# A two-layer trunk on one core: residual by token, MLPs with stationary activations, the up projection as Strassen's 2x2 product run in turns with the down projection

## The chip, the core and the metric

The kernel runs on one core of a Trainium2 chip. The core has a matrix engine (TensorE, PE in the profile, its weight loads PEld), VectorE (DVE), ScalarE (ACT), GpSimd (POOL) and SyncE (SP), and 16 DMA engines behind queues that SP and POOL write to. The metric is device time in microseconds (us) of one execution; lower is better.

## The reference, cut to what matters

256 tokens, 2048 channels, 8192 MLP channels, all float32. Layer 0 mixes by pooling, layer 1 by stick-breaking attention with 16 heads of 128; both end in a squared-ReLU MLP.

```
def squared_relu_mlp(x, w_up, w_down):
    h = jax.nn.relu(jnp.einsum('bsd,df->bsf', x, w_up))
    return jnp.einsum('bsf,fd->bsd', h * h, w_down)

x = x + multiscale_pool_mixer(rms_norm(x, pool_norm[0]), pool_w[0], pool_scale[0])
x = x + squared_relu_mlp(rms_norm(x, mlp_norm[0]), w_up[0], w_down[0])
kv = rms_norm(x, kv_norm) @ w_kv                  # [256, 4096]
q = rms_norm(x, attn_norm[0]) @ w_q
x = x + stick_breaking_attention(q, k, v) @ w_o[0]
x = x + squared_relu_mlp(rms_norm(x, mlp_norm[1]), w_up[1], w_down[1])
return rms_norm(x, final_norm)
```

## The kernel before

All weights come as blocks of 1 MB: 512 input channels by 512 output channels, on chip `[128, 4, 512]`. There are 324: 4 for pooling, 64 up and 64 down for each layer, 48 for K, Q and V, 16 for the attention's output projection (o_w). The list `order` fixes their sequence, and `emit_block` takes them from it, three ahead of the one in use (`AHEAD`): a DMA on SP's queue into `raw` (four buffers), then ACT copies it rounded into `hi` (L117) and DVE writes the rest, `raw - hi`, into `lo` (L118), in halves of 1024 columns. Activations too are split in two, side by side in one tile (`xt`, `ht`, `oT`: 256 columns of the high part, 256 of the low). A product is the sum of three: high by high, high by low, low by high.

The residual stream `xs[n]` lies transposed: channels on the partitions, 256 tokens in the columns. Two functions multiply:

- `product_w`, for up, down, K, Q and o_w: pieces of the weights are stationary (loaded into PE) and the activations stream. Each of 16 pieces of a block takes a matmul of 512 columns with `hi` (L158) and one of 256 with `lo` (L163).
- `product_a`, for the pooling map and V: pieces of the activations are stationary and 512 weight columns stream, 24 matmuls for a block (L196 to L198).

An MLP goes in groups of `GF` = 2048 hidden channels (`NG` = 4): four column tiles of up, of four blocks each, then four of down. The evacuation of an up tile adds the halves, applies the token scale and ReLU, squares and splits (`squared_relu`). The evacuation of a down or o_w tile adds to `xs` (`add_to_stream`, L289 and L290); in the last group it also makes the next product's activations, pair by pair (`Norm.take`). The norm's factor, 1 / rms, is put on behind the product.

Matmul order on PE, the order on each queue and the buffers are as the code is written, apart from what stands in `high_priority`. The line numbers are those of the profile.

Of the kernel before, what the change touches and what calls it, by code (L numbers as in the profile page):

```python
# [2 lines left out]

# [20 lines left out]
GF = 2048  # L24
# [6 lines left out]
AHEAD = 3  # L31
WARM = 12
COLS = ("pool", "mlp0", "mlp1", "kv", "attn", "pool_scale", "final")


@with_exitstack
def trunk_kernel(ctx: ExitStack, tc: tile.TileContext, xt_in, band, cols, pool_w, up_w, down_w,
                 k_w, q_w, v_w, o_w, out):
    """The residual stream lies transposed on chip: xs[n] is [channel, channel tile, token]."""
    nc = tc.nc  # L40

    const = ctx.enter_context(tc.tile_pool(name="const", bufs=1))
    wraw = ctx.enter_context(tc.tile_pool(name="wraw", bufs=4))
# [35 lines left out]
    order = []  # L79
    for g in range(NCH):  # L80
        order.append((pool_w[g], None))

    def mlp_blocks(layer):
        for g in range(NG):
            for n in range(NCH):
                for kg in range(NCH):
                    order.append((up_w[layer, g * NCH + n, kg], None))
            for n in range(NCH):
                for kg in range(NCH):
                    order.append((down_w[layer, g, n, kg], None))  # L90
# [12 lines left out]
    state = {"emitted": 0, "used": 0}

    def emit_block():
        i = state["emitted"]
        src, gain = order[i]
        raw = wraw.tile([P, KT, NB], F32, name="raw")
        step = KT // 2 if i < NCH else KT
        for k in range(0, KT, step):  # L110
            nc.sync.dma_start(raw[:, k:k + step, :], src[:, k:k + step, :])
        hi = whi.tile([P, KT, NB], F32R, name="hi")
        lo = wlo.tile([P, KT, NB], F32R, name="lo")
        if gain is None:
            step = KT // 2
# [29 lines left out]
    def product_w(acts, evacuate, groups=NCH):  # L145
        """bank[j] = rows of output tile j of (W.T @ x_hi + W_lo.T @ x_hi | W_hi.T @ x_lo)"""
# [24 lines left out]
    def summed(new_pair, then):  # L171
        """Evacuation that hands on the sums of two tiles' halves."""
# [11 lines left out]

    def product_a(acts, evacuate, groups=NCH):
        """bank[t] = tokens t's rows of acts.T @ W"""
        banks = [ps_w.tile([P, NB], F32, name="bank") for _ in range(NT)]
        for kg in range(groups):
            hi, lo = next_block()
            for t in range(NT):  # L190
                for k in range(KT):
                    a_hi = acts[kg][:, k, t * P:(t + 1) * P]
                    a_lo = acts[kg][:, k, S + t * P:S + (t + 1) * P]
                    first = kg == 0 and k == 0
                    last = kg == groups - 1 and k == KT - 1
                    nc.tensor.matmul(banks[t], lhsT=a_hi, rhs=hi[:, k, :], start=first, stop=False)  # L196
                    nc.tensor.matmul(banks[t], lhsT=a_lo, rhs=hi[:, k, :], start=False, stop=False)  # L197
                    nc.tensor.matmul(banks[t], lhsT=a_hi, rhs=lo[:, k, :], start=False, stop=last)  # L198
                if kg == groups - 1:
# [3 lines left out]
    def split_scaled(dst, k, src, gs):  # L203
        """the two float32r parts of src * gs"""
        nc.scalar.activation(out=dst[:, k, 0:S], in_=src, func=AF.Copy, scale=gs)
        nc.vector.scalar_tensor_tensor(out=dst[:, k, S:2 * S], in0=src, scalar=gs,
                                       in1=dst[:, k, 0:S].bitcast(F32), op0=ALU.mult,
                                       op1=ALU.subtract)
# [17 lines left out]
    class Norm:  # L226
        def __init__(self, gain):
            self.gain = gain
            self.xt = [None] * NCH
            self.acc = None  # L230
            self.halves = []

        def take(self, n, j):
            """Tile j of chunk n is complete."""
            if j % 2:
                ks = slice(j - 1, j + 1)
                self.parts(n, ks)
                self.squares(n, ks)

        def squares(self, n, ks):  # L240
            src = xs[n][:, ks, :]
            if self.acc is None:
                self.acc = small.tile([P, 2, S], F32, name="acc", bufs=1)
                nc.scalar.activation(out=self.acc, in_=src, func=AF.Square)
            else:
                sq = small.tile([P, 2, S], F32, name="sq", bufs=1)
                nc.scalar.activation(out=sq, in_=src, func=AF.Square)
                nc.vector.tensor_tensor(out=self.acc, in0=self.acc, in1=sq, op=ALU.add)

        def parts(self, n, ks):  # L250
            if ks.start == 0:
                self.xt[n] = xtpool.tile([P, KT, 2 * S], F32R, name="xt")
# [389 lines left out]
```

## Time and profile before

| | us |
|---|---|
| median of 3 runs | 1892.77 |
| the runs | 1892.1 to 1893.23 |
| span of the profiled execution | 1891.3 |
| PE busy in the span | 1873.9 |
| DVE busy | 1146.3 |
| ACT busy | 899.2 |
| POOL busy | 18.7 |

The span is the profiled execution from its first to its last instruction. Matmuls overlap each other in the records, so PE's busy time counts stretches, not the sum of durations.

### The profile page before, as it was taken

The page shows a single profiled execution, that of the slowest core. Times are in us where ns is not written, and L with a number is a line of the kernel's source. Part 1 is how long each engine was busy: PE and PEld are TensorE (multiplying, and loading weights), DVE is VectorE, ACT ScalarE, POOL GpSimd, SP SyncE. Part 2 cuts the span into 40 slices and gives each one's busy share as a digit, 9 for nine tenths or more (in the row PEclk, how much of TensorE's full clock was granted, in tenths as well). Part 3 has the DMA queues.
Part 4 walks back from the last instruction along what each step waited for, and adds up shares of the span by engine and source line. Part 5 has one row for each costly group of instructions (what it writes and reads, how often), then busy time and mean ns, then how long its engine had stood idle before and what let it go on. Part 6 is the DMA issues. An engine that isn't in the chain of part 4 may idle for free.

```text
span 1891.3 us, 25396 instructions
## 1 busy us (share of the span) xinstructions
PE 1873.9 (99%) x10496; PEld 1623.7 (86%) x10496; DVE 1146.3 (61%) x1546; ACT 899.2 (48%) x1229; POOL 18.7 (1%) x39
## 2 busy tenths in 40 slices
PE   8999999999999999999999999999999999999997
PEld 6888888888888888888888888888888888888886
DVE  8765555556655566675676666555565555655655
ACT  7643345335434444565665545443444345435443
POOL 0000000000000000000000100000000000000000
PEclk9999999999999999999999999999999999999999
DMA  7455555555554555544444454555555545555551
GB/s 285 178 179 198 181 186 192 180 192 185 180 197 181 181 198 180 183 173 178 158 177 178 160 196 178 180 199 179 192 185 181 195 180 187 191 181 183 194 182 63
DMA packets 49650, 346.40 MB, mean 183 GB/s; under 512 B 5632, under 2 KB 5888, under 8 KB 8576
## 3 DMA queue, kind: packets, MB, share of 16 engines
q1 hardware_dynamic: 49536, 344.80, 50.7%
q8 instruction: 82, 1.34, 0.3%
q14 instruction: 32, 0.26, 0.0%
HBM read 342.68 MB, written 2.10 MB: 182 GB/s over the span
## 4 chain that ended last, share of the span: by engine, by line
PE 98%; DVE 1%; DMA 0%; ACT 0%; issue 0%; SPq 0%; DVEq 0%
PE bank L158 60%; PE bank L163 31%; PE bank L196 2%; PE bank L197 2%; PE bank L198 2%; PE bank_m L472 0%; DMA raw<-in_pool_w 0%; PE bank_m L520 0%; PE bank_m L324 0%; DVE xs L569 0%; PE bank_m L497 0%; PE bank_m L522 0%; PE bank_m L474 0%; PE bank_m L326 0%; DVE lo L118 0%
## 5 line engine op out<-in xcount | busy, mean ns | idle before, releaser
L118 DVE TENSOR_TENSOR lo<-raw,hi 128x1024 fp32r<-128x1024 f32 x552 | 653.1, 1222 | 588.3 <-ACT hi L117 588.1
L117 ACT CAST hi<-raw 128x1024 fp32r<-128x1024 f32 x552 | 552.9, 1048 | 742.4 <-PE bank L158 532.3
L158 PE MATMUL bank<-xt,hi 128*128 128x512 f32 x2560 | 894.7, 398 | 0.0
L158 PE MATMUL bank<-ht,hi 128*128 128x512 f32 x2048 | 714.5, 396 | 0.0
L163 PE MATMUL bank<-xt,lo 128*128 128x256 f32 x2560 | 694.0, 281 | 0.0
L158 PEld LDWEIGHTS bank<-xt,hi 128*128 128x128 f32 x2560 | 471.0, 188 | 103.8
L163 PE MATMUL bank<-ht,lo 128*128 128x256 f32 x2048 | 555.7, 281 | 0.0
L163 PEld LDWEIGHTS bank<-xt,lo 128*128 128x128 f32 x2560 | 483.5, 189 | 13.7
L158 PEld LDWEIGHTS bank<-ht,hi 128*128 128x128 f32 x2048 | 376.3, 188 | 81.5
L163 PEld LDWEIGHTS bank<-ht,lo 128*128 128x128 f32 x2048 | 384.6, 188 | 11.8
L125 DVE SCALAR_TENSOR_TENSOR lo<-raw,gt,hi 128x512 fp32r<-128x512 f32 x192 | 135.3, 752 | 81.9 <-ACT hi L124 81.7
L124 ACT ACTIVATE hi<-raw,gt 128x512 fp32r<-128x512 f32 x192 | 125.4, 714 | 100.4 <-PE bank L158 55.6
L158 PE MATMUL bank<-oT,hi 128*128 128x512 f32 x256 | 89.2, 395 | 0.0
L179 ACT COPY s<-bank 128x256 f32<-128x256 f32 x128 | 46.8, 365 | 51.1 <-PE bank L158 51.1
L163 PE MATMUL bank<-oT,lo 128*128 128x256 f32 x256 | 69.6, 282 | 0.0
L196 PE MATMUL bank<-hi,xt 128*128 128x512 f32 x160 | 64.3, 402 | 4.5 <-ACT hi L117 4.5
L289 DVE TENSOR_TENSOR xs<-bank,xs 128x256 f32<-128x256 f32 x144 | 57.0, 416 | 12.7 <-PE bank L158 10.3
L197 PE MATMUL bank<-hi,xt 128*128 128x512 f32 x160 | 63.2, 395 | 0.0
L198 PE MATMUL bank<-lo,xt 128*128 128x512 f32 x160 | 63.1, 395 | 0.0
L400 DVE TENSOR_TENSOR ht<-q,ht 128x512 fp32r<-128x512 f32 x64 | 44.0, 688 | 28.3 <-ACT q L399 28.3
L290 DVE TENSOR_TENSOR xs<-bank,xs 128x256 f32<-128x256 f32 x144 | 57.4, 418 | 2.1
L158 PEld LDWEIGHTS bank<-oT,hi 128*128 128x128 f32 x256 | 47.0, 188 | 10.0
(106 smaller groups left out, 733.8 us busy)
## 6 DMA issues: line engine op xcount, KB each, us to landing
raw<-in_up_w SPq DMA_DIRECT2D x128, 1024.0 KB, 4.8
raw<-in_down_w SPq DMA_DIRECT2D x128, 1024.0 KB, 4.8
raw<-in_k_w SPq DMA_DIRECT2D x16, 1024.0 KB, 4.8
raw<-in_q_w SPq DMA_DIRECT2D x16, 1024.0 KB, 4.8
raw<-in_v_w SPq DMA_DIRECT2D x16, 1024.0 KB, 4.8
raw<-in_o_w SPq DMA_DIRECT2D x16, 1024.0 KB, 4.8
raw<-in_pool_w SPq DMA_DIRECT2D x8, 512.0 KB, 9.9
out_y<-xs SPq DMA_DIRECT2D x7, 256.0 KB, 2.3
```

Of the source, the lines that this page charges most:

```text
L117: nc.scalar.copy(out=hi[:, k:k + step, :], in_=raw[:, k:k + step, :])
L118: nc.vector.tensor_tensor(out=lo[:, k:k + step, :], in0=raw[:, k:k + step, :], in1=hi[:, k:k + step, :].bitcast(F32), op=ALU.subtract)
L124: nc.scalar.activation(out=hi[:, k, :], in_=raw[:, k, :], func=AF.Copy, scale=gs)
L125: nc.vector.scalar_tensor_tensor(out=lo[:, k, :], in0=raw[:, k, :], scalar=gs, in1=hi[:, k, :].bitcast(F32), op0=ALU.mult, op1=ALU.subtract)
L158: nc.tensor.matmul(banks[j], lhsT=hi[:, k, cols], rhs=a, start=first, stop=last)
L163: nc.tensor.matmul(banks[j][:, 0:S], lhsT=lo[:, k, cols], rhs=a[:, 0:S], start=False, stop=False)
L179: nc.scalar.copy(out=s, in_=bank[:, S:2 * S])
L196: nc.tensor.matmul(banks[t], lhsT=a_hi, rhs=hi[:, k, :], start=first, stop=False)
L197: nc.tensor.matmul(banks[t], lhsT=a_lo, rhs=hi[:, k, :], start=False, stop=False)
L198: nc.tensor.matmul(banks[t], lhsT=a_hi, rhs=lo[:, k, :], start=False, stop=last)
L289: nc.vector.tensor_tensor(out=dst, in0=bank[:, 0:S], in1=dst, op=ALU.add)
L290: nc.vector.tensor_tensor(out=dst, in0=bank[:, S:2 * S], in1=dst, op=ALU.add)
```

## The change

- **Residual by token.** `xr[t]` holds 128 tokens in the partitions and 2048 channels in the columns. What needs channels on partitions is transposed on PE, 128 by 128 at a time (`turned`, `turn`, `by_tokens`), and squares for the norm are summed by ACT.
- **Down and o_w** go with activations stationary, 24 matmuls of 512 columns for a block (`by_token`).
- **Up** is a 2x2 product of matrices of blocks (two halves of the tokens, of the channels, and of the group's 1024 columns) done in seven products, P1 to P7, in place of eight. Each product has two halves (P40 is half 0 of P4), and a half takes a 1 MB block of weights and 12 matmuls of 512 columns. `Fast.make` forms the seven activation sums. The weight sums are formed by DMA: tiles `c0`, `c1`, `d0` and `d1` hold a block of weights, and the next block is added to it by a transfer with `accum_op` on POOL's queue, after the split of the previous content (`CHAIN`). Of a group's 14 loads eight are of this kind; the rest, and the down blocks, go by SP. The host only lays out the weights in another order.
- **Turns.** A group has 1024 hidden channels (`NG` = 8). In stages 1 to 7 the halves of up alternate with four steps of transposing (T0 to T3) and eight blocks of the group before's down product (D00 is column tile 0, half 0). Stage 0 has up alone, stage 8 only T and D.
- **Buffers.** `raw` 3, loads four ahead, splits two ahead and 2048 columns in one instruction.

```diff
-GF = 2048
+GF = 2 * NB
...
-AHEAD = 3
+RAW = 3
+LOADS = 4
+SPLITS = 2
...
+SLOT = {1: 0, 2: 1, 3: 2, 5: 3, 7: 4, 6: 5, 4: 6}
+PARTS = 7
...
+CHAIN = {4: ("c", (1, 1), False), 5: ("c", (1, 0), True), 6: ("c", (0, 0), True),
+         3: ("c", (0, 1), True), 1: ("d", (0, 0), False), 7: ("d", (1, 0), True),
+         2: (None, (0, 1), False)}
+def stage_plan(g):
+    if g == 0:
+        order = "P40 P10 P50 P41 P11 P51 P60 P61 P70 P71 P30 P31 P20 P21"
+    elif g < NG:
+        order = ("T2 P40 T3 P41 T0 P10 T1 P11 D00 D01 P50 P51 D10 D11 P60 P61 D20 P70 P71 D21 "
+                 "P30 P31 D30 P20 P21 D31")
+    else:
+        order = "T0 T2 T1 T3 D00 D01 D10 D11 D20 D21 D30 D31"
+    return [(s[0], *map(int, s[1:])) for s in order.split()]
...
-            for n in range(NCH):
-                for kg in range(NCH):
-                    order.append((up_w[layer, g * NCH + n, kg], None))
-            for n in range(NCH):
-                for kg in range(NCH):
-                    order.append((down_w[layer, g, n, kg], None))
+        for g in range(NG + 1):
+            for what, a, *b in stage_plan(g):
+                if what == "D":
+                    block(down_w[layer, g - 1, a, b[0]])
+                elif what == "P":
+                    tag, (i, j), add = CHAIN[a]
+                    block(up_w[layer, g, i, j, b[0]], tag=tag and f"{tag}{b[0]}", add=add)
...
+    def load():
+        i = state["loaded"]
+        src, _, tag, base = order[i]
+        if base is not None:
+            while state["split"] <= base:
+                split()
+            raw = raws[base]
+            nc.gpsimd.dma_start(raw, src, accum_op=ALU.add)
+        else:
+            raw = wide(tag) if tag else wraw.tile([P, KT, NB], F32, name="raw")
+            step = KT // 2 if i < NCH else KT
+            for k in range(0, KT, step):
+                nc.sync.dma_start(raw[:, k:k + step, :], src[:, k:k + step, :])
...
+        while state["loaded"] < min(state["used"] + LOADS, len(order)):
+            load()
+        while state["split"] < min(state["used"] + SPLITS, len(order)):
+            split()
...
+        def turned(self, n, half, order):
+            bank = self.new_bank().rearrange("p (t k s) -> p t k s", t=NT, k=2)
+            for i, t in enumerate(order):
+                for k in range(2):
+                    c = n * NB + (2 * half + k) * P
+                    nc.tensor.transpose(bank[:, i, k, :], xr[t][:, c:c + P], ident)
+            return bank
...
+            for i in range(2):
+                nc.vector.tensor_tensor(out=f[:, 4 + i], in0=f[:, 1 + 2 * i], in1=f[:, 0],
+                                        op=ALU.subtract)
+            nc.vector.scalar_tensor_tensor(out=f[:, 6], in0=f[:, 4], scalar=-1.0, in1=f[:, 3],
+                                           op0=ALU.mult, op1=ALU.subtract)
+            nc.vector.tensor_tensor(out=f[:, 7], in0=f[:, 6], in1=f[:, 2], op=ALU.add)
+            pool = tc.alloc_tile_pool(name=f"fast{n}", bufs=1, side="right", reuse_waits="tile")
+            self.pools.append(pool)
+            hi = pool.tile([P, PARTS, 2, P], F32R, name="fh")
+            lo = pool.tile([P, PARTS, 2, P], F32R, name="fl")
+            nc.scalar.copy(out=hi, in_=f[:, 1:])
+            nc.vector.tensor_tensor(out=lo, in0=f[:, 1:], in1=hi.bitcast(F32), op=ALU.subtract)
+            self.parts[n] = (hi, lo)
...
+            def product(i, part):
+                name = {1: "x", 6: "x", 7: "x", 5: "y", 3: "y", 2: "z", 4: "z"}[i]
+                begins = part == 0 and i in (1, 5, 2, 4)
+                if begins:
+                    bank[name] = ps_s.tile([P, NB], F32, name=name)
+                b = bank[name]
+                hi, lo = next_block()
+                for kg in range(2):
+                    fh, fl = norm.parts[2 * part + kg]
+                    for k in range(2):
+                        ah, al = fh[:, SLOT[i], k, :], fl[:, SLOT[i], k, :]
+                        wh, wl = hi[:, 2 * kg + k, :], lo[:, 2 * kg + k, :]
+                        ends = part == 1 and kg == 1 and k == 1
+                        nc.tensor.matmul(b, lhsT=ah, rhs=wh, start=begins and kg == 0 and k == 0,
+                                         stop=False, skip_group_check=True)
+                        nc.tensor.matmul(b, lhsT=al, rhs=wh, start=False, stop=False,
+                                         skip_group_check=True)
+                        nc.tensor.matmul(b, lhsT=ah, rhs=wl, start=False, stop=ends,
+                                         skip_group_check=True)
+                if part == 0:
+                    return
...
+                if i in (4, 1, 5, 6):
+                    nc.scalar.copy(out=new({4: "21", 1: "11", 5: "22", 6: "12"}[i]), in_=b)
+                elif i == 3:
+                    nc.vector.tensor_tensor(out=u["12"], in0=b, in1=u["12"], op=ALU.add)
+                    relu("12")
+                elif i == 2:
+                    nc.vector.tensor_tensor(out=u["11"], in0=b, in1=u["11"], op=ALU.add)
+                    relu("11")
+                else:
+                    nc.vector.tensor_tensor(out=u["21"], in0=u["21"], in1=b, op=ALU.subtract)
+                    relu("21")
+                    nc.vector.scalar_tensor_tensor(out=u["22"], in0=b, scalar=-1.0, in1=u["22"],
+                                                   op0=ALU.mult, op1=ALU.subtract)
+                    relu("22")
...
+            def turn(i):
+                a, ks = i // 2, slice(2 * (i % 2), 2 * (i % 2) + 2)
+                if i % 2 == 0:
+                    h[a] = hp.tile([P, KT, 2 * S], F32R, name=f"ht{a}")
+                b = ps_s.tile([P, NB], F32, name="turn").rearrange("p (k s) -> p k s", k=2)
+                for k in range(2):
+                    for t in range(NT):
+                        c = (2 * (i % 2) + k) * P
+                        nc.tensor.transpose(b[:, k, t * P:(t + 1) * P],
+                                            u[f"{a + 1}{t + 1}"][:, c:c + P], ident)
+                nc.scalar.activation(out=h[a][:, ks, 0:S], in_=b, func=AF.Square)
+                q = ev.tile([P, 2, S], F32, name="q")
+                nc.scalar.activation(out=q, in_=b, func=AF.Square)
+                nc.vector.tensor_tensor(out=h[a][:, ks, S:2 * S], in0=q,
+                                        in1=h[a][:, ks, 0:S].bitcast(F32), op=ALU.subtract)
+            def down(n, part, follow):
+                if part == 0:
+                    bank["d"] = [ps_w.tile([P, NB], F32, name="bank") for _ in range(NT)]
+                by_token(bank["d"], h[part], next_block(), part == 0, part == 1)
+                if part == 1:
+                    for t in range(NT):
+                        nc.vector.tensor_tensor(out=chunk(t, n), in0=bank["d"][t],
+                                                in1=chunk(t, n), op=ALU.add)
+                    if follow is not None:
+                        follow.take(n)
...
+            for g in range(NG + 1):
+                follow = None
+                if g == NG:
+                    norm.release()
+                    follow = following(new_bank)
...
+        for g in range(NCH):
+            product_a([xt[g]], mapped(g), groups=1)
+            if g == 0:
+                scaled_bands()
+            else:
+                mixed(g - 1)
+        for g in range(2):
+            by_tokens(g)
+        early.release()
+        mixed(NCH - 1)
+        for g in range(2, NCH):
+            by_tokens(g)
+        norm.rows(norm.ss)
```

**PE, in an MLP's up projection.** Before, the pieces of a block alternate between the two widths (`bank` is the PSUM output, then stationary or streaming tile and weight part):

```order
L163 MATMUL bank_1437<-ht_889,lo_1442 128x256
L158 MATMUL bank_1437<-ht_889,hi_1441 128x512
L163 MATMUL bank_1437<-ht_889,lo_1442 128x256
L158 MATMUL bank_1437<-ht_889,hi_1441 128x512
L163 MATMUL bank_1437<-ht_889,lo_1442 128x256
```

Now, in stage 1 of layer 0, the end of P40, the transposes T3 (`c21` and `c22` are hidden activations) and the start of P41:

```order
L430 MATMUL z_2032<-hi_1992,fh_446 128x512
L432 MATMUL z_2032<-hi_1992,fl_447 128x512
L434 MATMUL z_2032<-lo_1993,fh_446 128x512
L472 MATMUL turn_2051<-ident_85,c21_1520 128x128 [waits PE_49,Activation_49]
L472 MATMUL turn_2051<-ident_85,c22_1678 128x128
L472 MATMUL turn_2051<-ident_85,c21_1520 128x128
L472 MATMUL turn_2051<-ident_85,c22_1678 128x128
L430 MATMUL z_2032<-hi_2035,fh_515 128x512
L432 MATMUL z_2032<-hi_2035,fl_516 128x512
L434 MATMUL z_2032<-lo_2036,fh_515 128x512 [waits DVE_49]
```

All matmuls of the product have 512 columns, and four transposes stand between two halves.

**DVE, at the end of pooling.** Before, the first up blocks' `lo` come between the additions of the pooled result to the stream (L329) and the activations' low parts (L206):

```order
L329 SCALAR_TENSOR_TENSOR xs_0_114<-bank_m_345,gt_83,xs_0_114 128x256 [waits PE_49]
L329 SCALAR_TENSOR_TENSOR xs_0_114<-bank_m_359,gt_83,xs_0_114 128x256 [waits PE_49]
L118 TENSOR_TENSOR lo_378<-raw_375,hi_377 128x1024 [waits DMAHW0_49,Activation_49]
L329 SCALAR_TENSOR_TENSOR xs_0_114<-bank_m_345,gt_83,xs_0_114 128x256 [waits PE_49]
L206 SCALAR_TENSOR_TENSOR xt_352<-xs_0_114,gt_83,xt_352 128x256 [waits Activation_49]
```

Now the additions are L571; L393 to L397 form activation sums and L403 splits them; `lo_645` and `lo_664` are those of P10 and P50, and P40's stands in the row ahead of these:

```order
L571 SCALAR_TENSOR_TENSOR xs0_139<-mix_351,gt_80,xs0_139 128x256 [waits PE_49]
L393 TENSOR_TENSOR raw_358<-raw_358 128x256 [waits Activation_49] x2
L395 SCALAR_TENSOR_TENSOR raw_358<-raw_358 128x256 [waits DVE_49]
L571 SCALAR_TENSOR_TENSOR xs1_140<-mix_416,gt_80,xs1_140 128x256 [waits PE_49]
L397 TENSOR_TENSOR raw_358<-raw_358 128x256 [waits DVE_49]
L571 SCALAR_TENSOR_TENSOR xs1_140<-mix_416,gt_80,xs1_140 128x256 [waits PE_49]
L182 TENSOR_TENSOR lo_645<-d0_382,hi_644 128x2048 [waits DMAHW1_49,Activation_49]
L403 TENSOR_TENSOR fl_375<-raw_358,fh_374 128x1792 [waits Activation_49]
L571 SCALAR_TENSOR_TENSOR xs1_140<-mix_423,gt_80,xs1_140 128x256 [waits PE_49]
L393 TENSOR_TENSOR raw_430<-raw_430 128x256 [waits Activation_49]
L571 SCALAR_TENSOR_TENSOR xs1_140<-mix_423,gt_80,xs1_140 128x256 [waits PE_49]
L182 TENSOR_TENSOR lo_664<-c0_310,hi_663 128x2048 [waits DMASW0_49,Activation_49]
```

The last `lo` waits for an adding transfer, and the additions for two more chunks of channels stand behind it.

**POOL's queue, stage 0 of layer 0.** Before, it carries no DMA. Now the first eight adding transfers are, in its order, those of P50, P70, P60, P51, P71, P61, P30 and P31:

```order
L163 DMA c0_310<-in_up_w 128x2048 [waits DMAHW7_49,DVE_49,PE_49]
L163 DMA d0_382<-in_up_w 128x2048 [waits DMAHW1_49,DVE_49,PE_49]
L163 DMA c0_310<-in_up_w 128x2048 [waits DMASW0_49,DVE_49]
L163 DMA c1_642<-in_up_w 128x2048 [waits DMAHW0_49,DVE_49]
L163 DMA d1_661<-in_up_w 128x2048 [waits DMAHW2_49,DVE_49]
L163 DMA c1_642<-in_up_w 128x2048 [waits DMASW3_49,DVE_49]
L163 DMA c0_310<-in_up_w 128x2048 [waits DMASW2_49,DVE_49]
L163 DMA c1_642<-in_up_w 128x2048 [waits DMASW5_49,DVE_49]
```

Each waits for DVE, which has to be done with the tile's `lo`, and from the third on most wait for an earlier adding transfer (DMASW).

## Rows read from the trace of the kernel before

**Rows 1.** The page: busy time, chain that ended last, one kind of load.

```profile
PE 1873.9 (99%) x10496; PEld 1623.7 (86%) x10496; DVE 1146.3 (61%) x1546; ACT 899.2 (48%) x1229; POOL 18.7 (1%) x39
...
PE 98%; DVE 1%; DMA 0%; ACT 0%; issue 0%; SPq 0%; DVEq 0%
...
raw<-in_up_w SPq DMA_DIRECT2D x128, 1024.0 KB, 4.8
```

**Rows 2.** Windows: length; PE, PEld, DVE, ACT, POOL busy; clock, DMA share, GB/s.

```profile
10.00:20.00 10.00, 10.00 (x35) 8.04 (x36) 8.68 (x14) 8.75 (x17) 0.00 (x0) 0.79 1.02 415
20.00:30.00 10.00, 10.00 (x47) 8.14 (x46) 9.04 (x16) 9.48 (x19) 0.00 (x0) 1.00 0.93 374
...
40.00:400.00 360.00, 360.00 (x2046) 313.47 (x2045) 217.05 (x283) 162.12 (x210) 0.00 (x0) 1.00 0.52 184
```

**Rows 3.** Timeline of PE in a V block (`product_a`): start, duration, instruction.

```profile
831.06 0.39 PE L196 MATMUL bank<-hi,xt 128*128 128x512 f32 x1
...
833.55 0.40 PE L198 MATMUL bank<-lo,xt 128*128 128x512 f32 x1
```

**Rows 4.** Lines, shapes apart: busy, mean ns; idle time before and its releaser.

```profile
L118 DVE TENSOR_TENSOR lo<-raw,hi 128x1024 fp32r<-128x1024 f32 x552 | 653.1, 1222 | 588.3 <-ACT hi L117 588.1
L117 ACT CAST hi<-raw 128x1024 fp32r<-128x1024 f32 x552 | 552.9, 1048 | 742.4 <-PE bank L158 532.3 <-issue 204.7 <-PE bank L197 3.5
...
L400 DVE TENSOR_TENSOR ht<-q,ht 128x512 fp32r<-128x512 f32 x64 | 44.0, 688 | 28.3 <-ACT q L399 28.3
L399 ACT ACTIVATE q<-u 128x512 f32<-128x512 f32 x64 | 39.6, 619 | 0.0
```

**Rows 5.** Timeline of PE, short matmuls: pooling, then sums for a norm.

```profile
36.46 0.38 PE L326 MATMUL bank_m<-bands,y 128*128 128x128 f32 x2
36.68 0.60 PE L324 MATMUL bank_m<-bands,y 128*128 128x256 f32 x2
...
780.00 0.59 PE L273 MATMUL bank_m<-half,ones 128*128 128x256 f32 x2
780.43 0.50 PE L281 MATMUL bank_m<-ones,half 128*128 128x1 f32 x4
780.80 0.36 PE L163 MATMUL bank<-xt,lo 128*128 128x256 f32 x1
```

**Rows 6.** Timeline of PE at the start; the last row is the MLP's first matmul.

```profile
9.88 0.79 PE L196 MATMUL bank<-hi,xt 128*128 128x512 f32 x1 [4.52 <-ACT hi L117]
...
13.46 0.63 PE L196 MATMUL bank<-hi,xt 128*128 128x512 f32 x1
13.89 0.57 PE L197 MATMUL bank<-hi,xt 128*128 128x512 f32 x1
...
14.53 0.40 PE L196 MATMUL bank<-hi,xt 128*128 128x512 f32 x1
14.76 0.39 PE L197 MATMUL bank<-hi,xt 128*128 128x512 f32 x1
...
38.43 0.48 PE L158 MATMUL bank<-xt,hi 128*128 128x512 f32 x1
```

**Rows 7.** Timeline of DVE at the start: pooling bands scaled, first addition to stream.

```profile
31.19 1.93 DVE L310 TENSOR_SCALAR bands<-bands,rows 128x256 f32<-128x256 f32 x8
...
35.30 0.87 DVE L329 SCALAR_TENSOR_TENSOR xs<-bank_m,gt,xs 128x256 f32<-128x256 f32 x2
```

**Rows 8.** Timeline at the end: last product matmul, last multiplications.

```profile
1877.74 0.40 PE L158 MATMUL bank<-ht,hi 128*128 128x512 f32 x1
...
1882.90 4.71 DVE L569 TENSOR_TENSOR xs<-xs,rb 128x256 f32<-128x256 f32 x9
```

**Rows 9.** Waits of SP's queue: total us, times, longest.

```profile
SPq L111 <- DVE lo L118: 1073.8, 203, 10.6
```

More of the change, by code (lines that the diff above doesn't have):

```diff
@@ L188, in product_a @@
         for kg in range(groups):
[L189 to L199, printed above, removed]
+            by_token(banks, acts[kg], next_block(), kg == 0, kg == groups - 1)
+            if kg == groups - 1:
+                for t in range(NT):
                     evacuate(t, banks[t])
             after_block()
[L203 to L208, printed above, removed]
     def rsqrt_mean(ss, shape, name):
-        r = small.tile(shape, F32, name=name, bufs=1)
+        r = small.tile(shape, F32, name=name)
         nc.scalar.activation(out=r, in_=ss, func=AF.Ln, scale=1.0 / D, bias=eps)
-        ms = small.tile(shape, F32, name=f"{name}_ms", bufs=1)
+        ms = small.tile(shape, F32, name=f"{name}_ms")
         nc.vector.tensor_scalar(out=ms, in0=ss, scalar1=1.0 / D, scalar2=EPS, op0=ALU.mult,
@@ L223, in rsqrt_mean, with chunk @@
         return r
+    xr = [xpool.tile([P, D], F32, name=f"xr{t}") for t in range(NT)]
+    def chunk(t, n):
+        return xr[t][:, n * NB:(n + 1) * NB]
     class Norm:
[L227 to L238, printed above, removed]
@@ new lines, in rows, with per_column @@
+        def rows(self, ss):
+            total = small.tile([P, NT], F32, name="total")
+            nc.vector.tensor_reduce(out=total, in_=ss, axis=AX.X, op=ALU.add)
+            self.r = rsqrt_mean(total, [P, NT], "rows")
+        def per_column(self, pool, bank):
+            for t in range(NT):
+                diag = pool.tile([P, P], F32, name="diag")
+                nc.vector.tensor_scalar(out=diag, in0=ident, scalar1=self.r[:, t:t + 1],
+                                        scalar2=None, op0=ALU.mult)
+                nc.tensor.matmul(bank[:, t * P:(t + 1) * P], lhsT=ones, rhs=diag, start=t == 0,
+                                 stop=t == NT - 1)
+            rb = pool.tile([P, S], F32, name="rb")
+            nc.scalar.copy(out=rb, in_=bank[:, 0:S])
+            return rb
@@ L313, in mapped @@
         def mapped(g):
+            ys[g] = [pp.tile([P, NB], F32, name=f"y{t}") for t in range(NT)]
             def go(t, bank):
-                nc.scalar.copy(out=ys[t][g], in_=bank)
+                nc.scalar.copy(out=ys[g][t], in_=bank)
             return go
@@ L332, in mixed, with by_tokens @@
                                                    op1=ALU.add)
-                    norm.take(g, h + k)
+            norm.make(g, xs[g])
+        def by_tokens(g):
+            for t in range(NT):
+                bank = new_bank()
+                for k in range(KT):
+                    nc.tensor.transpose(bank[:, k * P:(k + 1) * P], xs[g][:, k, t * P:(t + 1) * P],
+                                        ident)
+                nc.scalar.copy(out=chunk(t, g), in_=bank)
+            norm.squares(g)
         def load_stream(n, pieces=1):
@@ L338, in load_stream @@
                 nc.sync.dma_start(xs[n][:, k:k + step, :], xt_in[n, :, k:k + step, :])
[L340 to L346 removed]
         load_stream(0, 2)
+        nc.sync.dma_start(gt, cols)
         all_parts(0)
[L350 removed]
+        load()
+        split()
         all_squares(0)
@@ L353, in trunk_kernel @@
         all_parts(1)
-        emit_block()
+        load()
+        split()
         all_squares(1)
```

414 lines of the change are left out of this document (225 added, 189 removed).

## The prediction

> **What bounds the kernel now.** I read the page first: PE is busy 99% of the span, and the chain of work that ended last runs over PE for 98% [rows 1]. Nothing else is near: DVE stands at 61%, ACT at 48%. The groups by line say why those two idle: 588 of DVE's idle microseconds end with ACT's `hi`, 532 of ACT's with PE giving a bank or buffer free [rows 4], and SP's queue, which issues the loads, stood 1074 us waiting for `lo` to give a `raw` buffer free [rows 9]. So loads and splits run as far ahead as buffers allow and wait for PE. In the windows, 40 to 400 us has PE busy in all 360 us at the full clock, the DMA engines at 0.52 [rows 2]. PE's time is the kernel's time, so I price the change on PE first, and then ask where PE would newly wait.
>
> **Prices on PE.** A block by `product_w` is 32 matmuls; 2046 in 360 us are 63.9 blocks, so 5.63 us each [rows 2]. By `product_a` eleven steps take 833.55 − 831.06 = 2.49 us, 0.2264 each [rows 3]: a block of 24 takes 5.43 us, a half of 12 takes 2.72. A short float32 matmul with its own weight load costs little: the pair of 128 columns takes 36.68 − 36.46 = 0.22, so 0.11; the four sums take (780.80 − 780.43)/4 = 0.093 [rows 5]. A transpose is that shape, 128 by 128; I take 0.10 (both rows as bounds).
>
> **Terms on PE.** Against the profiled execution's span of 1891.3 us (the median of the runs is 1.5 above it, and I keep that offset):
> - Up: 128 blocks × 5.63 = 720.6 become 2 × 8 × 14 = 224 halves × 2.72 = 609.3: **−111**. Seven products in place of eight give 1/8, and the shorter stationary side the rest.
> - Down and o_w: 144 blocks × (5.63 − 5.43): **−29**. K, Q and V stay.
> - Transposes: T0 to T3 are 16 each group, 256 in all; the K/Q/V and second MLP's activations take 64: 320 × 0.10 = **+32**. Those in pooling and at the end belong to terms below.
> - The column and row sums for norms in mid-run go (0.43 and 0.37 at 780 [rows 5], twice): **−2**.
>
> Were PE never to wait, 1891.3 − 110 = 1781.
>
> **What feeds PE in a mid-group.** There are 14 (two layers, stages 1 to 7). PE has 14 × 2.72 + 8 × 5.43 + 16 × 0.10 = 83 us of work. DVE: a `lo` in two halves takes 2 × 1.222; in one instruction the fixed part falls away once (from 512 to 1024 columns, 0.688 to 1.222 [rows 4], that part is 0.154), so 2.29; 22 of them, and 16 of 512 columns at 0.69 (adds to the stream, evacuation, low parts), give 61 us. ACT: 22 × 1.9 (worked out in the same way) and 16 × 0.62 [rows 4], 52 us. Both fit, and neither is above three quarters.
>
> DMA is less clear. At saturation, 415 and 374 GB/s at shares of 1.02 and 0.93 [rows 2], a full share is 405 GB/s: 1 MB takes 2.6 us. A group has 14 plain loads, 36 us, and 8 adding ones, a kind of transfer that the trace of before does not have. If adding costs like one copy: 57 us; as it has to read the weights and what lies in the tile, two copies are natural: 78 us, 94% of 83; at three, 98 us. PE has to wait from (83 − 36)/21 = 2.24 copies on. Bounds 1 and 3, I take 2. The Trainium skill, "Collectives: The Full Stack", "Why ReduceScatter is half of AllGather" (Part 3), says that an adding transfer is held back by its two source reads and not by the addition, with a measured ratio of 1.93; by it the group's transfers would take 76 us. No row here shows it.
>
> Inside such a group a new wait could come at the T steps. There is one `turn` bank: T1 waits until ACT has squared T0's twice (1.24 [rows 4]), and D00 waits for T1's low part; the P half between them covers most of 0.62 × 2 + 0.69. I take 0.6 a group, **+8** (0 if covered; 2 × 1.93 a group, +54, if not). In the last stage of each layer T0, T2, T1, T3 stand in a row with nothing between: four times about 1.24, less what PE does, 4 a layer: **+8**.
>
> **Start.** Before, PE begins the MLP at 38.4 [rows 6], for the blocks' `lo` slip in between the stream's additions. Now all four chunks have to be mixed, turned and have their sums formed, and the order on DVE puts the `lo` of P50 in the middle of the additions. That one waits for an adding transfer, which waits for the `lo` of P40; behind it stand two chunks' additions and sums, and PE's last transposes in front of P40 wait for these. From the scaled bands (33.1 [rows 7]) DVE has 16 additions × 0.44 [rows 7], two pooling `lo` halves (2.4), the `lo` of P40, P10 and P50 (6.9), four activation sums for each of four chunks at about that 0.44, and four splits of 1792 columns at 2.0: 31 us, of which the last chunk's sums and split may fall behind P40's start, so 26: 59. The `lo` of P50 can't start before P40's `lo` (about 38), a transfer of 4.8 as the plain ones [rows 1] to twice that, and ACT's 1.9, so not before 45 to 50; the queue gets there at about 47. That, DVE's waits for ACT's parts of each sum, and the last transposes are 7 more: P40 starts at about 66, **+28**. Bounds: +18 (no wait, and one more chunk behind P40) and +40 (P50's transfer late by twice its length).
>
> **Stage 0.** Fourteen halves are 38 us of PE's work, but their weights hang together: P50 to P61 to P31 are links that each need landing, `hi` and `lo` before the next transfer may start. A link is about 4.8 to 6 + 1.9 + 2.3 [rows 1, 4], 10 us. POOL's queue keeps its order, and P51 is issued behind P60, which waits for P50's `lo`. So P50 10, P51 10, P61 10, P31 10, and three halves (P31, P20, P21) 8.2 behind: 49 us. Twice 49 − 38 = 11: **+22** (bounds +10, if transfers of the two chains overlap, and +45, with 15 us links).
>
> **Seams.** Where the stream's new columns feed a norm (last stage into K/Q/V, o_w into the second MLP, last stage into the end), the transposes for a chunk wait for DVE's two additions, 2 × 0.69, and stand on PE before the next block: about 1 each, eleven with work behind: **+11** (0 to 20). **End**: four transposes, copies and the factor come behind the last matmul, where 13.6 us stood (1891.3 − 1877.7 [rows 8]): **+1.5**.
>
> **Clock.** After 4.5 us without work PE's first steps at 9.9 us stand 0.43 apart (13.46 to 13.89) and from 14.5 on 0.23 [rows 6]; the granted clock of that window is 0.79 [rows 2], a mixture of 1.2 and 2.4 GHz. Some ten steps at 0.2 more: 2 us for a stall of that length. Two such stalls in the above: **+4** (up to 9). The Trainium skill, "TensorE: Matmul & The Clock Gate", "Part 1: The HAM clock gate", has the clock halved after idling and earned back by work; that speaks against a change that makes PE wait, and the rows agree. [...]
>
> **Sum.** −110 + 8 + 8 + 28 + 22 + 11 + 1.5 + 4 = −27.5: a span of 1864, a run of **1865 us**. With all low bounds of waits (0, 4, 18, 10, 0, 0, 0) it is 1813; the high ones do not come together, but start and stage 0 at their highest give +35 and 1900.
>
> **Rivals.**
> - *Adding transfers cost three copies.* Then DMA bounds each mid-group: 98 us against 83, 15 × 14 = 210, and stage 0's links get longer by 5 us, 20 a layer: about 2110. It decides from about 2.35 copies, where 14 × (36 + 21 × 2.35 − 83) eats my 27. For it: the price isn't in the trace, the tile is also one of DMA's two inputs. Against: three is a read more than adding needs. Chance 0.10.
> - *PE waits for splits in mid-groups.* Splits run two blocks ahead, with whole 2048 columns, three `hi` and `lo`; a half's 2.72 us is hardly above a `lo` of 2.29, so a row of P halves leaves DVE 0.4 spare each, and a late adding transfer holds DVE's queue with all evacuations behind it. 3 us a group are +42: about 1907, slower. It decides at 2 us a group, 28 in all. For it: before, with 5.63 us a block, DVE had twice the room. Against: the 8 D blocks of 5.43 give DVE 25 us of room in each group, and the P halves stand between them in most places. Chance 0.22.
> - *The waits are hidden*: an adding transfer costs little over one copy, links overlap and the start loses 18: about 1830 (1813 to 1840). Chance 0.15.
> - *Gains and losses cancel*, within 0.2%: start and stage 0 towards their upper bounds, +28 beyond mine. Chance 0.06.
>
> My forecast (1840 to 1889) has 0.47. A difference of 0.2%, 3.8 us, is about what a measurement of this kernel can tell from no change. Faster than 1889: 0.47 + 0.15 = 0.62; the same 0.06; slower 0.32. The range leaves out the three-copy case and half of the tails, 0.2 in all: 1815 to 1930.
>
> **What would show it.** Chain: PE's share falls from 98 to about 93%. P halves at 2.72 apart, P40 first at about 66 us; each stage 0 lasts near 49 with PE waiting for `hi` and `lo`; a middle group 84 to 86. The adding transfers' time to landing under load and the DMA share in mid-groups (0.9 for two copies, 0.7 for one, 1.0 with PE waiting for three) decide the first rival; PE's idle time before L430 and L434 inside stages 1 to 7 the second. I am wrong if middle groups last over 87 us, or if P40 starts before 50 or after 80.

## The result, and the profile after

The changed kernel takes 1914.7 us (four runs, 1914.3 to 1915.6) against 1892.8: a ratio of 1.0116, interval 1.0102 to 1.0131. It is 22 us slower, where 1865 was forecast; the time lies inside the range, on the side that I gave 0.32.

The page of the kernel after: busy times, the DMA queues (q1 is SP's, q0 GpSimd's), the chain, and the up loads with their time to landing.

```profile
PE 1851.8 (97%) x8372; PEld 1497.3 (78%) x8372; DVE 1267.5 (66%) x1071; ACT 1109.8 (58%) x1125; POOL 130.9 (7%) x169
...
q1 hardware_dynamic: 44928, 311.24, 44.0%
q0 software_dynamic: 18432, 134.23, 35.2%
...
PE 86%; issue 8%; DMA 3%; ACT 1%; DVE 1%; POOL 0%; SPq 0%; DVEq 0%; POOLq 0%; ACTq 0%
...
c<-in_up_w POOLq DMA_DIRECT2D x96, 1024.0 KB, 10.2
c<-in_up_w SPq DMA_DIRECT2D x32, 1024.0 KB, 5.0
```

Only 22 us of PE's busy time are gone against [rows 1], where the prediction's terms on PE came to 110. The windows of its stretches (start; stage 0, stages 1 to 7 and stage 8 of the first MLP; K to o_w; the same stages of the second; the end):

```profile
0.00:71.50 71.50, 60.50 (x267) 46.83 (x268) 43.42 (x76) 51.70 (x98) 4.11 (x12) 0.86 0.71 218
71.50:129.60 58.10, 46.45 (x171) 35.32 (x171) 33.67 (x26) 33.00 (x32) 4.96 (x6) 0.85 0.86 230
129.60:732.10 602.50, 601.13 (x2633) 483.04 (x2632) 421.40 (x267) 355.38 (x267) 47.80 (x56) 1.00 0.92 264
732.10:786.10 54.00, 51.83 (x235) 40.78 (x234) 31.34 (x38) 29.23 (x49) 0.00 (x0) 0.97 0.47 162
786.10:1181.50 395.40, 390.12 (x2029) 330.75 (x2027) 253.06 (x339) 226.25 (x342) 20.37 (x34) 1.00 0.53 180
1181.50:1241.30 59.80, 48.12 (x169) 36.65 (x170) 34.60 (x27) 31.20 (x26) 5.78 (x7) 0.83 0.89 225
1241.30:1844.20 602.90, 601.33 (x2633) 482.97 (x2632) 421.23 (x267) 355.15 (x267) 47.88 (x56) 1.00 0.92 264
1844.20:1897.20 53.00, 50.34 (x235) 39.83 (x234) 21.69 (x19) 24.99 (x40) 0.00 (x0) 1.00 0.23 80
1897.20:1912.30 15.10, 2.00 (x12) 1.17 (x10) 7.06 (x17) 2.94 (x9) 0.00 (x0) 0.69 0.38 139
```

| stretch, us | before | after | difference |
|---|---|---|---|
| until the first MLP matmul | 38.4 | 71.5 | +33.1 |
| first MLP | 730.1 | 714.6 | −15.5 |
| K to o_w | 386.5 | 395.4 | +8.9 |
| second MLP | 722.7 | 715.7 | −7.0 |
| end | 13.6 | 15.1 | +1.5 |

(The bounds of the stretches are good to 0.4 us. Before, the first MLP also held some 7.5 us of pooling's matmuls.) By the prediction's terms the two MLPs should have given some 66 us (−111 − 26 + 26 + 16 + 22 + 7); they gave 22. In stages 1 to 7 PE is busy at the full clock in all but 1.4 to 1.6 of 602.5 and 602.9 us, 86 us a group. So hardly anything waits there, and it is the work that is longer. The timeline of PE in V, and in the up projection of the same run:

```profile
833.38 0.39 PE L258 MATMUL bank<-hi,c 128*128 128x512 f32 x1
...
836.10 0.39 PE L258 MATMUL bank<-hi,c 128*128 128x512 f32 x1
...
331.11 0.40 PE L434 MATMUL y<-lo,fh 128*128 128x512 f32 x1
...
332.51 0.40 PE L434 MATMUL y<-lo,fh 128*128 128x512 f32 x1
```

Twelve steps of V take 2.72 us, 0.2267 each, as in [rows 3]; six of up take 1.40, 0.2333 each, though the matmul has the same shape. Down, which stands on the very lines of V (L258 to L261), has 0.2334, o_w 0.2333. A group has 360 such steps: 84.0 us, and 16 transposes of 0.11 make 85.8.

### The profile page after: what moved, and what is told of

Same layout as the page of the kernel before. It is cut to its first block, busy times and chain, and to the rows that moved or that the text cites. A ratio compares the mean times of both kernels' runs of the same rounds, so it can differ in the third digit from the quotient of the medians.

```text
span 1912.3 us, 21042 instructions
## 1 busy us (share of the span) xinstructions
PE 1851.8 (97%) x8372; PEld 1497.3 (78%) x8372; DVE 1267.5 (66%) x1071; ACT 1109.8 (58%) x1125; POOL 130.9 (7%) x169
## 3 DMA queue, kind: packets, MB, share of 16 engines
q0 software_dynamic: 18432, 134.23, 35.2%
## 4 chain that ended last, share of the span: by engine, by line
PE 86%; issue 8%; DMA 3%; ACT 1%; DVE 1%; POOL 0%; SPq 0%; DVEq 0%; POOLq 0%; ACTq 0%
PE bank L260 14%; PE bank L261 14%; PE bank L258 14%; PE bank L224 6%; PE x L434 4%; PE x L430 4%; PE x L432 4%; PE bank L229 3%; PE y L430 3%; PE y L432 3%; PE y L434 3%; PE z L430 3%; PE z L434 3%; PE z L432 3%; DMA c<-in_up_w 3%
## 5 line engine op out<-in xcount | busy, mean ns | idle before, releaser
L182 DVE TENSOR_TENSOR lo<-raw,hi 128x2048 fp32r<-128x2048 f32 (+1 forms) x184 | 412.8, 2245 | 211.8 <-ACT hi L181 211.7
L181 ACT CAST hi<-raw 128x2048 fp32r<-128x2048 f32 (+1 forms) x184 | 345.4, 1878 | 284.8 <-PE bank L260 198.3
L182 DVE TENSOR_TENSOR lo<-c,hi 128x2048 fp32r<-128x2048 f32 x128 | 293.1, 2290 | 190.9 <-ACT hi L181 190.7
L260 PE MATMUL bank<-hi,ht 128*128 128x512 f32 x1024 | 406.5, 398 | 0.8 <-DVE ht L477 0.8
L258 PE MATMUL bank<-hi,ht 128*128 128x512 f32 x1024 | 402.9, 395 | 4.0 <-ACT ht L474 4.0
L261 PE MATMUL bank<-lo,ht 128*128 128x512 f32 x1024 | 406.3, 397 | 0.2 <-DVE lo L182 0.2
L181 ACT CAST hi<-c 128x2048 fp32r<-128x2048 f32 x128 | 245.1, 1915 | 210.9 <-DMA c<-in_up_w 93.0
L260 PEld LDWEIGHTS bank<-hi,ht 128*128 128x128 f32 x1024 | 192.3, 188 | 53.2 <-DVE ht L477 6.0
L258 PEld LDWEIGHTS bank<-hi,ht 128*128 128x128 f32 x1024 | 192.2, 188 | 50.4 <-ACT ht L474 4.9
L261 PEld LDWEIGHTS bank<-lo,ht 128*128 128x128 f32 x1024 | 192.4, 188 | 44.5 <-DVE lo L182 0.6
L430 PE MATMUL x<-hi,fh 128*128 128x512 f32 x384 | 156.4, 407 | 10.4 <-ACT hi L181 10.4
L432 PE MATMUL x<-hi,fl 128*128 128x512 f32 x384 | 155.0, 404 | 0.0
```

The lines of the kernel that those rows point to most:

```text
L181: nc.scalar.copy(out=hi[:, k:k + step, :], in_=raw[:, k:k + step, :])
L182: nc.vector.tensor_tensor(out=lo[:, k:k + step, :], in0=raw[:, k:k + step, :], in1=hi[:, k:k + step, :].bitcast(F32), op=ALU.subtract)
L430: nc.tensor.matmul(b, lhsT=ah, rhs=wh, start=begins and kg == 0 and k == 0, stop=False, skip_group_check=True)
L432: nc.tensor.matmul(b, lhsT=al, rhs=wh, start=False, stop=False, skip_group_check=True)
```

## Experiments

"Aligned" below means with the gaps of e1_align. Steps are mean distances of successive starts in unbroken runs of the timeline.

**e1_align, e2_offsets, e8_offsets: where the tiles lie.** In the built program the activations' tiles lie at a distance from the `hi` and `lo` tiles that is, modulo 512 bytes, 0 for V and pooling, 160 for `ht` and `oT`, 384 for `fh` and `fl`. My theory A: this makes the step.

```diff
+    right = ctx.enter_context(tc.tile_pool(name="right", bufs=1, side="right"))
...
+    nc.vector.memset(right.tile([P, 96], F32, name="gap_r"), 0.0)
+    nc.vector.memset(xpool.tile([P, 88], F32, name="gap_x"), 0.0)
```

> Unused gaps of 352 and 384 bytes a partition shift the tiles of activations (ht, oT, fh, fl), so that they lie like V's, a multiple of 512 bytes from the hi and lo tiles; nothing else changes. Theory A (the step between matmuls depends on how the stationary tile lies against the moving one): the 0.2333 us steps of up, down and o_w become V's 0.2267, 5760 + 384 steps x 0.0067 = 41 us less, 1874 us. Theory B (V's faster step comes from the lighter traffic around it, the narrower splits, or its short stretches): steps stay at 0.233, time 1912 to 1917.

> Gaps that lay the tiles at other distances: V and pooling at 448 bytes modulo 512 (was 0), down and o_w at 128 (was 160), up at 256 (was 384). Theory A: V's steps, which were 0.2267, become 0.233 or so; one of the others may get faster, if a distance of 128 or 256 is enough. Theory B: V stays at 0.2267 and the others at 0.233.

e1_align took 1883.4 us, a ratio of 0.9946 to the kernel before (0.9931 to 0.9960): 31 less than after. The timeline of PE in down:

```profile
331.49 0.39 PE L261 MATMUL bank<-hi,ht 128*128 128x512 f32 x1
...
334.89 0.39 PE L261 MATMUL bank<-hi,ht 128*128 128x512 f32 x1
```

Fifteen steps in 3.40 us, 0.2267. The whole stretch of stages 1 to 7 falls from 602.5 to 591.1 in the first MLP and from 602.9 to 589.3 in the second. e2_offsets (1905.0) and e8_offsets (1899.8), one run each, put the tiles elsewhere:

> The kernel after the change with other gaps: V and pooling at 128 bytes modulo 512, down and o_w at 256, up at 64. If a multiple of 256 bytes is what makes the step short: down and o_w 0.227 (0 and 256 were fast), V 0.233 (128 and 384 were slow), up between them at 0.229 (as V at 448).

| distance, bytes modulo 512 | step, us |
|---|---|
| 0 | V 0.2278, up 0.2276, down 0.2269, o_w 0.2272 |
| 256 | up 0.2278 (e2), down 0.2279 (e8) |
| 448 | V 0.2291 (e2) |
| 128 | V 0.2322 (e8), down 0.2327 (e2) |
| 64 | up 0.2334 (e8) |
| 160, 384 | down 0.2334, up 0.2329 (after) |

The rows of 0 are those of e1_align. V in e8, 21 steps in 4.88 us, 0.2324 each:

```profile
826.74 0.39 PE L263 MATMUL bank<-hi,c 128*128 128x512 f32 x1
...
831.62 0.39 PE L263 MATMUL bank<-hi,c 128*128 128x512 f32 x1
```

Distances alone make V slower and the others faster, so the rival (traffic, split widths, short stretches) falls. It is the distance and not one tile's place: in e1 only the activations' tiles moved, in e2 and e8 V's stayed and `hi` and `lo` moved. 0 and 256 are fast. Two misses: V at 448 has 0.2291 where 0.233 or so was expected, and 64 is as slow as any. e1's forecast of 1874 was missed by 9 us; it took the 0.2267 of twelve steps for V's step, and over all its unbroken runs V has 0.2278.

K and Q, with weights stationary, don't show the effect: a step of 512 columns and one of 256 together take 0.351 to 0.353 us at 0 (after, e1), at 448 (e2) and at 128 (e8), and 0.352 to 0.353 in the kernel before. So no run gives a reason to expect the same gain from gaps in the kernel before; it was not tried.

**e3_stage0, e4_no_add: what holds stage 0.** It takes 58 and 60 us, with 39 of work. In the first of them PE stands idle for 11.6 us, each time for a `hi` or `lo`. The longest of these waits, on ACT and then on PE:

```profile
88.21 1.90 ACT L181 CAST hi<-c 128x2048 fp32r<-128x2048 f32 x1 [4.58 <-DMA c<-in_up_w]
...
90.16 0.61 PE L430 MATMUL y<-hi,fh 128*128 128x512 f32 x1 [4.43 <-ACT hi L181]
```

```diff
-        order = "P40 P10 P50 P41 P11 P51 P60 P61 P70 P71 P30 P31 P20 P21"
+        order = "P40 P10 P41 P11 P50 P20 P51 P21 P60 P70 P61 P71 P30 P31"
```

```diff
-            nc.gpsimd.dma_start(raw, src, accum_op=ALU.add)
+            nc.gpsimd.dma_start(raw, src)
```

> Stage 0 in the order P40 P10 P41 P11 P50 P20 P51 P21 P60 P70 P61 P71 P30 P31, so that at least four halves (11 us) stand between two links of a chain in place of two. Theory A (stage 0 waits for its links of landing, hi, lo): its 58 and 60 us fall to about 48 each, 1893 us in all. Theory B (splits or plain loads hold it): within 3 us of 1915.

> The transfers on GpSimd's queue copy in place of adding, with the same waits (so the weight sums are left out of the computation). Theory A (adding costs two copies, and is hidden except in stage 0's links): landing 5 us in place of 10, stage 0 shorter by 3 links x 4 = 12 us a layer, stages 1 to 7 unchanged at 85.8 us each, 1890 us. Theory B (stages 1 to 7 are held by the transfers): they get shorter by over 2 us each, below 1865 us.

e3 (in whose order P6's sum takes in half of P7, so part of the result is another) took 1920.3 us, a ratio of 1.0143 (1.0127 to 1.0160). Stage 0 fell only to 55.7 and 57.1, and stage 1 grew by 6.2 and 4.3. The windows of it (second stage 0, and 25 us inside it):

```profile
1182.90:1240.00 57.10, 45.91 (x168) 34.93 (x169) 31.68 (x25) 29.05 (x24) 5.19 (x6) 0.85 0.95 250
1190.00:1215.00 25.00, 18.02 (x72) 13.84 (x71) 13.98 (x7) 11.61 (x9) 3.46 (x4) 0.88 1.00 262
```

There the DMA engines have a share of 1.00 at 262 GB/s, where plain loads reached 415 [rows 2]. e4 took 1899.1 (one run), with stage 0 at 49.6 and 52.4. Its page:

```profile
q0 software_dynamic: 18432, 134.23, 20.3%
...
c<-in_up_w POOLq DMA_DIRECT2D x96, 1024.0 KB, 5.2
```

So adding costs the kernel 16 us, nearly all in stage 0, as theory A of e4 has it, though 8.4 and 7.4 in place of its 12 a layer. e3's theory A falls as it was put: more halves between two links don't bring stage 0 to 48.

**e6_align_order, e7_order_no_add: latency or volume.** Aligned, order `P40 P10 P41 P11 P50 P20 P51 P21 P60 P61 P70 P71 P30 P31`, with and without adding.

> As e1_align, with stage 0 in the order P40 P10 P41 P11 P50 P20 P51 P21 P60 P61 P70 P71 P30 P31. Theory A (the links' latency holds stage 0): 56 and 59 us fall to about 46. Theory B (the volume holds it: six plain loads at 2.7 and eight adding ones at 5.26 are 58 us of the DMA engines): within 3 us of 56 and 59, or what is won there is lost in stages 1 to 7; time 1880 to 1887 us.

> As e6_align_order, but the transfers on GpSimd's queue copy in place of adding (the weight sums are left out of the computation). Theory A (latency): the same as e6. Theory B (volume): with 14 x 2.7 = 38 us of transfers neither volume nor links hold stage 0 any more: about 42 us, 14 less than e6, a span of 1855.

One run each: 1884.3 and 1856.1. The windows of both stages 0, e6 and then e7:

```profile
69.20:124.70 55.50, 44.76 (x170) 34.70 (x170) 30.55 (x24) 30.63 (x30) 4.29 (x5) 0.88 0.87 242
1165.30:1219.90 54.60, 43.88 (x168) 34.12 (x169) 31.52 (x25) 28.53 (x24) 5.19 (x6) 0.87 0.98 254
```

```profile
72.40:118.30 45.90, 40.73 (x170) 32.31 (x170) 30.67 (x24) 30.73 (x30) 2.64 (x5) 0.96 0.79 291
1151.30:1196.00 44.70, 40.35 (x168) 32.00 (x169) 31.63 (x25) 28.85 (x24) 3.17 (x6) 0.96 0.81 302
```

Stage 1 (from its first transpose to the next stage's, as in the other stages) tells where the waiting goes, and stages 2 to 7 take the same throughout: 85.8 us a group in after, e3 and e4, and 83.8 in the aligned ones apart from e9 and e10 (99 to 105).

| us, first and second MLP | stage 0 | stage 1 |
|---|---|---|
| after | 58.0, 59.8 | 87.5, 87.9 |
| e1_align | 56.4, 58.8 | 88.3, 86.5 |
| e3_stage0 | 55.7, 57.1 | 93.7, 92.2 |
| e4_no_add | 49.6, 52.4 | 87.5, 87.5 |
| e6_align_order | 55.5, 54.6 | 93.7, 92.2 |
| e7_order_no_add | 45.9, 44.7 | 85.6, 85.6 |
| e11_vector_half | 47.2, 46.8 | 94.9, 94.1 |
| e12_vector_all | 47.9, 53.1 | 99.1, 98.9 |

With adding, the order only moves the wait into stage 1; with plain transfers it helps (e7 against e4, although e7 is aligned too). So it is the adding that holds stage 0. Whether by volume or by later landing isn't parted: without adding both go, and in the first stage 0 a transfer into `c` lands in 5.6 us (e4) in place of 8.1 (after; medians). Volume isn't the whole of it. In after's stages 0 the DMA engines have shares of 0.86 and 0.89, so 50 and 53 us of transfers in 58 and 60, and near the start of the first they stand almost idle:

```profile
74.50:78.00 3.50, 3.50 (x17) 2.84 (x16) 2.62 (x4) 3.47 (x7) 0.00 (x0) 1.00 0.14 56
```

For volume speak the share of 1.00 in e3 and stage 1 of e11 (below).

**e5_align_mix: the start.** `pd = ps_w.tile([P, 2, S], F32, name="bank")` in place of `ps_m`'s `mix`, aligned.

> As e1_align, and the pooled result at the start goes through the four product banks in place of a single bank of its own. Theory A (the start waits in a chain from bank to bank: matmul, addition, matmul): P40 starts at about 63 us in place of 72, 1875 us. Theory B (DVE's queue with three lo and the activation sums in it sets P40's start): 72 us, 1883 us.

1888.2 us, a ratio of 0.9972 (0.9959 to 0.9984), 5 us slower than e1; P40 starts at 74.4. Theory A falls. In the kernel after DVE's timeline shows P50's `lo` between the additions:

```profile
54.30 0.48 DVE L571 SCALAR_TENSOR_TENSOR xs<-mix,gt,xs 128x256 f32<-128x256 f32 x1 [1.31 <-PE mix L568]
54.70 2.28 DVE L182 TENSOR_TENSOR lo<-c,hi 128x2048 fp32r<-128x2048 f32 x1
```

That fits theory B, which was not tried by itself, and whose 72 and 1883 us were not met either.

**e9_pool_adds, e10_pool_order: sums on GpSimd.** Aligned; e10 with e6's order.

```diff
-            nc.gpsimd.dma_start(raw, src, accum_op=ALU.add)
+            new = wraw.tile([P, KT, NB], F32, name="raw")
+            nc.sync.dma_start(new, src)
+            nc.gpsimd.tensor_tensor(out=raw, in0=raw, in1=new, op=ALU.add)
```

> As e1_align, with the weight sums formed on GpSimd: all blocks load by SP as plain copies, and a GpSimd addition of 128x2048 adds the new block to the link's tile. Theory B of e6 (the volume of the adding transfers holds stage 0): without them stage 0 is left with its links, 50 to 53 us as without adding (e4), if an addition takes some 4 to 5 us, eight times what a GpSimd pass over 256 columns took (0.5 to 0.7): about 1872 us. If the additions are slower than 9 us, eight of them are over 72 us a group, PE waits in stages 1 to 7, over 1890.

> As e9_pool_adds, with the order of stage 0 as in e6. If volume and links together held stage 0 (e6, e7): 45 to 47 us, 1858 to 1862 us in all, 1.7% under the kernel before. If the GpSimd additions take too long: as in e9.

2147.4 and 2148.3 us, ratios of 1.1339 (1.1316 to 1.1362) and 1.1348 (1.1329 to 1.1367). A clear miss. The groups by line of e9:

```profile
L168 POOL TENSOR_TENSOR c<-c,raw 128x2048 f32<-128x2048 f32 x96 | 502.7, 5243 | 914.0 <-DMA raw<-in_up_w 616.8 <-DVE lo L187 162.0 <-DVE xr L491 78.7
...
L187 DVE TENSOR_TENSOR lo<-raw,hi 128x2048 fp32r<-128x2048 f32 x176 | 555.4, 3168 | 125.7 <-ACT hi L186 125.6
```

An addition takes 5.2 us (5.8 for `d`), near the 4 to 5 expected, but GpSimd stands 617 us waiting for loads, which now share three `raw` buffers with everything else, and `lo` takes 3.17 us in place of the 2.29 of after:

```profile
L182 DVE TENSOR_TENSOR lo<-raw,hi 128x2048 fp32r<-128x2048 f32 x176 | 403.1, 2291 | 206.3 <-ACT hi L181 206.2
```

PE itself waits most for DVE, 108 us for `lo` and 47 for `ht`. Which of the two, loads or the slower DVE, costs more was not tried.

**e11_vector_half, e12_vector_all: sums of stage 0 on VectorE.** Aligned, e6's order; e12 for both halves.

```diff
+                          vector=add and g == 0 and b[0] in (1,))
...
+        if by_vector[i]:
+            nc.vector.tensor_tensor(out=raw, in0=raw, in1=extra[i], op=ALU.add)
```

> As e6_align_order, but in stage 0 of each layer the four sums of the second halves (P51, P61, P71, P31) are formed by VectorE from plain loads, in front of their splits; stages 1 to 7 keep the adding transfers. Volume of stage 0: 10 x 2.7 + 4 x 5.26 = 48 us, VectorE 34 + 4 x 2.3 = 43. If volume holds stage 0: 55 and 54.6 us fall to about 49 each, 1872 us. If latency of the first halves' links holds it: within 2 us of e6, 1883 us.

> As e11_vector_half, with all eight sums of stage 0 by VectorE. Volume 14 x 2.7 = 38 us, VectorE 34 + 8 x 2.3 = 52. If volume held stage 0, VectorE takes its place, about 52 us, 1878 us; with the links shorter by the adding transfers' 8 to 11 us it may come near e7's 45, 1860 us. If neither: 1883 us.

e11 takes 1875.0 us, a ratio of 0.9898 (0.9884 to 0.9913), the best of those that compute the whole; stage 0 is 47.2 and 46.8 us, where 49 were expected if volume holds it. That rules out the first halves' links as the sole limit, not the second halves', which got shorter along with the volume. e12 takes 1890.3, 0.9986 (0.9977 to 0.9995), a miss: its second stage 0 has 53.1, and in both a part of the gain goes again in stage 1 (the table). The windows of e11's stages 0, and of the part of stage 1 ahead of its longest wait:

```profile
72.30:119.50 47.20, 42.56 (x170) 33.12 (x169) 38.69 (x28) 29.05 (x30) 1.72 (x2) 0.93 0.85 276
1161.00:1207.80 46.80, 39.48 (x158) 30.62 (x159) 39.09 (x29) 27.26 (x23) 1.72 (x2) 0.93 0.84 268
119.50:163.00 43.50, 41.35 (x187) 33.32 (x185) 28.16 (x18) 26.34 (x23) 5.14 (x6) 1.00 0.98 255
```

In stage 1 ACT waits for two adding transfers, and PE for ACT, behind 43 us in which the DMA engines have a share of 0.98:

```profile
159.79 1.91 ACT L192 CAST hi<-c 128x2048 fp32r<-128x2048 f32 x1 [8.74 <-DMA c<-in_up_w]
...
167.16 1.90 ACT L192 CAST hi<-c 128x2048 fp32r<-128x2048 f32 x1 [4.98 <-DMA c<-in_up_w]
...
169.11 0.50 PE L441 MATMUL x<-hi,fh 128*128 128x512 f32 x1 [2.47 <-ACT hi L192]
```

e6 shows the same two waits, 8.55 and 5.04 us. A shorter stage 0 leaves stage 1 to wait for its adding transfers.

## Why the prediction was wrong

- **Price of a step** (0.2264 us, read from 2.5 us of V): this step failed. Over 5760 steps of the MLPs and 384 of o_w the 0.0069 up to 0.2333 are 42 us: up gave 128 × 5.63 − 224 × 2.80 = 93 in place of 111, down and o_w 4 in place of 29. Two errors make it. The eleven steps were a short sample: over all its unbroken runs V had 0.2277 in the kernel before, which is 0.0013 of the 0.0069, some 8 us. The other 0.0056, 34 us, is that the new tiles lie at other distances than V's; e1 gives 31 of them back.
- **Stage 0** (49 us): mis-sized, 58 and 60, 20 in all, of which 2 belong to the step. I had priced the links with a landing of 4.8 to 6 us; in these stages transfers into `c` took a median of 8.1 and 8.8. And I had set DMA's volume against the mid-groups, never against this stage: six plain and eight adding loads are 6 × 2.83 + 8 × 5.26 = 59 us (44.0% and 35.2% of 1912 us over 297 and 128 blocks). That this is just the stage's length is in part chance, for some of these loads run ahead of it. The runs show that adding is the term (e4, e7); which of the two sides of it stays open. My upper bound, +45, was too low by its own links: four of 15 us and 8.2 are 68, +60 in both.
- **Adding at two copies**: right, 5.26/2.83 = 1.86; against the plain transfers on GpSimd's own queue in e4 (20.3% of 1897 us over 128 blocks, 3.0 us) it is 1.75. The Trainium skill's 1.93 ("Collectives: The Full Stack", "Why ReduceScatter is half of AllGather"), measured there on collectives, is 4% above the first. The three-copies rival falls; the DMA share in mid-groups is 0.92, where 0.9 was to show two copies.
- **Mid-groups**: 85.8 us where 84 to 86 were to show it right, but that is luck: 83 of work and 0.6 of waiting had been forecast, and it is longer steps with no wait at T steps or splits from stage 2 on. That +8 did not come, and the rival at 0.22 (PE waits for splits) falls; its time, 1907, came nearest, by another cause. My two signs of being wrong (groups over 87 us, P40 before 50 or after 80) did not show, apart from stage 1's 87.5 and 87.9. What did show it are the P halves, 2.80 apart in place of 2.72, and PE's share of the chain, 86% in place of 93.
- **Start** +33 against +28, K to o_w +9 against +5 (−3 − 2 + 6 and seams of 4; o_w's longer steps are 2.6 of the rest), end +1.5: right within 6. Pooling's 7.5 us, which before stood inside the first MLP, are now in the start; I had added them there and not taken them off the MLP.
- **Clock**: PE busy in stage 0 is 46 and 48 us for 39 of work, at a granted clock of 0.85 and 0.83, a mixture of 1.2 and 2.4 GHz after waits: some 16 us more busy time in both, where I had 4 in all. How much of it lengthens the stage, and how much would have gone in waiting for loads, no run shows; in e7, with shorter waits, the clock is 0.96.

Together: 1864 + 42 + 18 + 5 − 8 − 8 − 4 = 1909, the span measured being 1912. The two eights are the T steps and pooling; the 4 is the clock's term, which the measured lengths of start and stage 0 already hold.

## What to carry to other kernels

Price a matmul step from many rows, with the same tiles' places, or allow for both; where a step differs by some 3% with no wait, look at the addresses. Set every transfer's volume against the stage that it falls into, not against the steady state. A transform that saves an eighth of the matmuls pays with what surrounds it: here the start cost 33 us and the waits of stage 0 some 40 (58 + 60 − 78), and aligned tiles, another order of stage 0 and four sums on VectorE turned +1.2% into −1.0%.

## What the runs showed of the hardware that was not expected

With activations stationary, the time between two like matmuls depended on the distance of the stationary tile from the moving one: 0.227 to 0.228 us at 0 and 256 bytes modulo 512, 0.229 at 448, and 0.232 to 0.2334 at 64, 128, 160 and 384. With weights stationary (K and Q) it did not, at 0, 128 and 448. Why is open. A transfer that adds took 1.86 times the engines' time of a plain load. A GpSimd addition of 128x2048 took 5.2 to 5.8 us, and in that run VectorE's subtraction of that size took 3.0 to 4.2 us on average, by tile, in place of 2.3.
